# Grouped-query heads of a two-layer diffusion step: four edits to where weight and output splits stand in the order

## The chip, the cores and the metric

The kernel runs on one core of one Trainium2 chip. The metric is the device time of one execution in microseconds, taken as the median of several runs. Beside the timed runs there is one profiled execution, whose trace is read here. Engines are named as in the profile: PE is TensorE, PEld its weight loads, DVE is VectorE, ACT is ScalarE, POOL is GpSimd and SP the engine whose queue issues most DMAs.

## The reference

One step of a transformer with two layers, for 512 latent tokens and 128 context tokens together (640 columns), model width 1024, all in float32. Layer 0 mixes with latent attention and neighbourhood attention, layer 1 with grouped-query attention; a gated feed-forward network follows each. The change lies in layer 1's mixer:

```python
def odd_mixer_latent(h, c_k, c_v, w_in, q_norm, k_norm, w_out, cos, sin):
    b, L, _ = h.shape
    q, k, v = odd_project(h, w_in, q_norm, k_norm)
    q = apply_rope(q, cos, sin)
    k = apply_rope(k, cos, sin)
    o = attend_blocked(q, jnp.concatenate([k, c_k], axis=1), jnp.concatenate([v, c_v], axis=1), GQA_SCALE)
    return o.reshape(b, L, -1) @ w_out
```

There are eight query heads of 128 and two heads of keys and values. `odd_project` multiplies by the input weights and normalises each query and key by its root mean square. The latent tokens read all latent tokens and 128 cached tokens (`c_k`, `c_v`); the context tokens read only themselves.

## The kernel before

Activations lie transposed, features on the 128 partitions and the 640 tokens along the free dimension, in two halves of 320. A float32 product is made of three matmuls: each operand is split into a rounded high part and a rest, and high times high, high times rest and rest times high are added up in PSUM (`mm3`). So every weight tile that arrives by DMA is split before it is used: `unit` (line 168) loads 128x1024 into a raw buffer, ScalarE copies the high part (line 173), VectorE subtracts for the rest (line 174). `rsplit` (line 458) does the same with an activation.

Buffers that matter here: three raw buffers (`rawp`, line 72), each given back when its subtraction is done; three split weight buffers (`wp`, line 73); eight high and eight rest activation tiles (`ring`, line 71).

The order within an engine is made beforehand by a list scheduler: the program order gives each instruction a rank, and the scheduler takes, by its own model of times, the first in rank whose inputs are there. On the chip each engine then runs its list strictly in order. Two helpers bind it further. `after(inst, fn)` (line 177) puts the instructions that `fn` makes for the engine of `inst`, and only those, behind `inst`. `run` (line 115) and `sequence` (line 121) chain pieces on TensorE: each piece's matmuls come behind those of the piece before.

The grouped-query layer goes through these stages:

- Keys. `two_halves` (line 1041) multiplies the two key weights, first for tokens 0 to 319, then for the rest; `knorm` (line 1733) normalises, rotates and splits the keys into `gkh` and `gkl`. The cached keys and values, of 128x256 each, are loaded (lines 1762 and 1765) and split into their places among the keys and values by `ksplit` and `gvsplit`.
- Values. `gvalues` (line 1711) multiplies two value weights, each of four of the eight feature tiles; they are fetched when `gvalues` first asks for them, and their ScalarE copies come behind a step of the activation that feeds the layer (line 1707). The order of the pieces is the list at line 1766.
- Heads. `gqa_q` (line 1782) makes a head's query in eight pieces (`q0` to `q7`), the first four for the first half of the tokens. When a half is done, ScalarE takes it out of PSUM (`gqc`), VectorE rotates it in four instructions (`gqr`), and it is split into `gqh` and `gql`. The sums of squares (`gsq`, then the matmuls `gr`) give the query's scale `rq`. The weight of head h is fetched at the head's first query piece, its ScalarE copy behind the first `gqc` of the head before (line 1783).
- Scores. `gqa_scores` (line 1809) has five blocks: four of 128 latent queries over 640 keys, and a fifth of the context tokens over themselves. Each goes through matmuls (`gs`), a maximum (`gn`), a bias (`gb`) and an exponential (`gp`, line 1833) with its sum, then a scaling on GpSimd. Two PSUM places serve them, so block j+2 waits for the exponential of block j.
- Values of a head. Transposes (`gt`) of the weighed scores are split into `gts_..h` and `gts_..l` and multiplied by the values (`go`); the output goes to `oG`. These pieces of head h run between the scores and queries of head h+1, in the order `GQA_ORDER` (line 1869). Head 7's run by themselves at the end (line 1881).
- Output. The eight outputs are split by `rsplit` (lines 1880 and 1882) into `oGs0` to `oGs7`, and `mixer_out` (line 1049) multiplies eight weights (`ocw0` to `ocw7`), one for each block of 128 output features (`oc0` and so on). The first two output blocks leave the last head's share for later. Between the blocks VectorE makes the last modulation vectors (`junk`, line 1630) from weights `wm` and a broadcast of the conditions (`cbo`), which are loaded on SP's queue among the output weights.

Around the edits the program has these lines:

```python
    ckf = load(cgkT, 256, "gckf")
    for v in range(2):
        ksplit(v, 512, 640, ckf[:, P * v:P * v + P])
    gvsplit(4, load(cgv, 256, "gcvf"))
    run([lambda: gvalues(range(2), range(KT)),
```

Of the kernel before, what the change touches and what calls it, by code (L numbers as in the profile page):

```python
# [13 lines left out]
AF = mybir.ActivationFunctionType  # L14
# [4 lines left out]
P = 128  # L19
# [32 lines left out]
def body(ctx, tc, xT, vecs, crow, wm0, wm0g1, wm0g, wm1, wA, wNV, wNA, wMK, wMV, wOA, wGQ, wGK, wGV, wOC,  # L52
# [3 lines left out]
    V, S, G = nc.vector, nc.scalar, nc.gpsimd  # L56
# [106 lines left out]
    def load(src, n, name):  # L163
        raw = rawp.tile([P, 1024], F32, tag="raw", name=name)
        nc.sync.dma_start(raw[:, :n], src)
        return raw[:, :n]

    def unit(src, n, name, lo="v", pool=None, bufs=3):

        raw = load(src, n, name + "r")  # L170
        t = (pool or wp).tile([P, 2, 1024], F32R, tag="w", bufs=bufs, name=name)
        hi, lw = t[:, 0, :n], t[:, 1, :n]
        S.activation(hi, raw, AF.Copy)
        (V if lo == "v" else G).tensor_tensor(lw, raw, f(hi), ALU.subtract)
        return hi, lw
# [307 lines left out]
    def lazy(fn):  # L483
        box = []

        def get():
            if not box:
                box.append(fn())
            return box[0]
        return get  # L490
# [555 lines left out]
                wh, wl = un(w0)  # L1046
                proj(pss[u][c], wh[0], wh[1], hh, hl, [k], *HALF[c], first=first and j == 0, last=last and j == n - 1, w0=wl)

    def mixer_out(wsrc, os_, order, xin, ml, name, nxt, pre, beside=None, early=False):

        nrm = Norm(name + "n", D)
        oh, ol = [o[0] for o in os_], [o[1] for o in os_]
        x = []
        ks = [(k, k) for k in order]
        if True:
            def wunit(n):
                get = lazy(lambda: unit(wsrc[n], 1024, f"{name}w{n}"))
                return lambda w0: (get(), w0)

            def evac(n, c, ps):  # L1060
                if c == 0:
                    x.append(xin(n))
                residual(x[n], x[n], ps, ml, G1, n, c)
                nrm.add(x[n], c)

            def half(ps, un, c, ks, first=True, last=True):
                two_halves([ps], [un], ks, oh, ol, c, first=first, last=last)

            held = []
            uns = [wunit(n) for n in range(KT)]  # L1070
            for n in range(KT):
                un = uns[n]
                if beside and n >= 1:
                    if early:
                        un(0)
                    beside(n - 1)
                if n < 2:
                    ps = pair(f"{name}{n}")
                    for c in range(2):
                        half(ps, un, c, ks[:-1], last=False)  # L1080
                    held.append((ps, un))
                    if n == 1:
                        for i, (ps, un) in enumerate(held):
                            for c in range(2):
                                half(ps, un, c, ks[-1:], first=False)
                                evac(i, c, ps[c])
                        held = []
                elif n < 5:
                    ps = pair(f"{name}{n}")
                    for c in range(2):  # L1090
                        half(ps, un, c, ks)
                        evac(n, c, ps[c])
                else:
                    ps = pair(f"{name}{n}") if n < 7 else [bank(f"{name}{n}{c}") for c in range(2)]
                    half(ps, un, 0, ks)
                    evac(n, 0, ps[0])
                    held.append((n, ps, un))
            pre()
            for j in range(KT - 2):
                for n, ps, un in held:  # L1100
                    half(ps, un, 1, ks[j:j + 1], first=j == 0, last=False)
                if j >= 1:
                    nxt(x, nrm, 0, (j - 1,))
            for i, (n, ps, un) in enumerate(held):
                half(ps, un, 1, ks[-2:], first=False)
                evac(n, 1, ps[1])
                nxt(x, nrm, 0, (5 + i,))
        return x, lambda: nxt(x, nrm, 1, range(KT))
# [650 lines left out]
    def gvsplit(i, src):  # L1759
        S.activation(gvh[i], src, AF.Copy)  # L1760
        V.tensor_tensor(gvl[i], src, f(gvh[i]), ALU.subtract)
    ckf = load(cgkT, 256, "gckf")
    for v in range(2):
        ksplit(v, 512, 640, ckf[:, P * v:P * v + P])
    gvsplit(4, load(cgv, 256, "gcvf"))
    run([lambda: gvalues(range(2), range(KT)),
         lambda: two_halves(pss, units, allk[:5], hh, hl, 1, last=False),
         lambda: knorm(0),
         lambda: two_halves(pss, units, allk[5:], hh, hl, 1, first=False),
         lambda: ksquare(1),  # L1770
         lambda: gvalues(range(2, 5), range(2)),
         lambda: knorm(1),
         lambda: gvalues(range(2, 5), range(2, KT))])
# [3 lines left out]
    S.activation(gvf[:, :256], gvo[4], AF.Copy)  # L1777
    nc.gpsimd.dma_start(o_gv, gvf[:, :256])

    gqs = {}  # L1780

    def gqa_q(h):
        get = lazy(lambda: after(gqs[h - 1][3][0] if h else None, lambda: unit(wGQ[h], 1024, f"wgq{h}")))
        qh = gp.tile([P, T], F32R, tag="gqh", bufs=2, name=f"gqh{h}")
        ql = gp.tile([P, T], F32R, tag="gql", bufs=2, name=f"gql{h}")
        rq = tiny.tile([P, 5], F32, tag="rq", bufs=2, name=f"rq{h}")
        sq = tmp(f"gsq{h}")
        gqs[h] = qh, ql, rq, []
        out = []
        for c, (c0, c1) in enumerate(HALF):  # L1790
            def done(ps, c=c, c0=c0, c1=c1):
                qc = tp.tile([P, HT], F32, tag="u", bufs=7, name=f"gqc{h}{c}")
                gqs[h][3].append(S.activation(qc, ps[:, :HT], AF.Copy))
                S.activation(sq[:, c0:c1], qc, AF.Square)
                qr = tp.tile([P, HT], F32, tag="u", bufs=7, name=f"gqr{h}{c}")
                rope(qr, qc, vcol(V_GQ), c, f"gqr{h}{c}")
                S.activation(qh[:, c0:c1], qr, AF.Copy)
                V.tensor_tensor(ql[:, c0:c1], qr, f(qh[:, c0:c1]), ALU.subtract)
            out += pieces_of(f"gq{h}{c}", qbank, get, hh, hl, list(range(KT)), c0, c1, done)

        def rstd():
            pr = bank(f"gr{h}")
            for j in range(5):
                PE.matmul(pr[:, 2 * j:2 * j + 2], sq[:, P * j:P * j + P], ones[:, 0:2], start=True, stop=True)
            S.activation(rq, pr[:, 0:10].rearrange("p (a b) -> p a b", b=2)[:, :, 0], AF.Ln, bias=eps, scale=1.0 / P)
            S.activation(rq, rq, AF.Exp, bias=lnsc, scale=-0.5)
        return out + [rstd]

    def gqa_scores(h, pts):
        v = h // 4  # L1810
        ll = tiny.tile([P, 5], F32, tag="lg", bufs=4, name=f"gl{h}")

        def piece(j):
            qh, ql, rq, _ = gqs[h]
            q = qh[:, P * j:P * j + P], ql[:, P * j:P * j + P]
            nm = tiny.tile([P, 1], F32, tag="nm", name=f"gn{h}_{j}")
            nb = tiny.tile([P, 1], F32, tag="nb", name=f"gb{h}_{j}")
            pss = bank2(f"gs{h}_{j}")
            if j < 4:
                pt = gp.tile([P, T], F32, tag="gp", bufs=8, name=f"gp{h}_{j}")  # L1820
                scores(pss, q, kTh[v], kTl[v])
                V.tensor_reduce(nm, pss[:, :, :HT], AX.XY, ALU.max, negate=True)  # L1822
                src, dst, n = pss[:, :, :HT], halves(pt), T
            else:
                pt = gp.tile([P, P], F32, tag="gpp", bufs=1, name=f"gp{h}_{j}")
                src = pss[:, 0, :P]
                mm3(src, *q, kTh[v][:, 640:768], kTl[v][:, 640:768], True, True)
                V.tensor_reduce(nm, src, AX.X, ALU.max, negate=True)
                dst, n = pt, P

            def weigh():
                V.tensor_tensor(nb, nm, rq[:, j:j + 1], ALU.mult)  # L1832
                S.activation(dst, src, AF.Exp, bias=nb, scale=rq[:, j:j + 1], accum_out=ll[:, j:j + 1])  # L1833
                softmax_tail(pt, ll[:, j:j + 1], f"gr{h}_{j}", n)
                pts.append(pt)
            return weigh

        box = []
        rest = {f"s{j}": (lambda j=j: piece(j)()) for j in range(1, 5)}
        return {"s0": lambda: box.append(piece(0)), "x0": lambda: box[0](), **rest}  # L1840
# [29 lines left out]
    for h in range(8):  # L1870
# [4 lines left out]
        if h < 7:  # L1875
# [1 line left out]
            pieces.update(named("q", qp))  # L1877
        sequence(GQA_ORDER, {**pieces, **tail})
        tail = gqa_values(h, pts, oG[h])
    oGs = [rsplit(oG[h], f"oGs{h}") for h in range(7)]  # L1880
    sequence("t0 t1 t2 v0 t3 pt v1 t4 v2 v3 v4 pv", tail)
    oGs.append(rsplit(oG[7], "oGs7"))
    sb.close()
# [3 lines left out]
    box, nxt = next_mod("h11", gs[1][1], mods[1], SH2, op[7])  # L1887
    _, before = mod_side([(1, wm1[G2:], G2)], None)
    x, pend = mixer_out(wOC, oGs, list(range(8)), lambda n, x=x: x[n], mods[1], "oc", nxt, op[-1],
                        before(op[5], op[5], (2, 1, 1, 2, 1, 1, 0)), True)  # L1890

    def final(x, nrm, c, ks, root):
        c0, c1 = HALF[c]
# [167 lines left out]
```

## Time and profile before

| | us |
|---|---|
| median of 3 runs | 1498.22 (1497.03 to 1499.88) |
| profiled execution, whole | 1497.4 |
| profiled execution, from first to last instruction (span) | 1495.3 |
| mean granted clock of TensorE in it | 0.996 |
| first matmul of the keys | 823.3 |
| first score matmul of head 0 | 863.8 |
| last query matmul of head 7 | 986.1 |
| first matmul of the output projection | 1001.0 |

How to read the lines quoted below. A row of a timeline gives the start in microseconds from the start of the span, the duration, the engine (PEq, SPq for a queue that issues a DMA), the line of the program, the operation, the tile written and the tiles read, the shape, the number of such instructions merged into the row, and in brackets the idle time of the engine before it with what ended it. Matmuls overlap: a matmul of 128x320 takes 0.31 us by its row while one starts every 0.15. A row of a table of windows gives a stretch of the span, its length, the busy time of PE, PEld, DVE, ACT and POOL with the number of instructions, the granted clock of TensorE, the share of DMA time and the GB/s.

### The profile page before, as it was taken

What the parts mean: (1) busy time and instruction counts of PE and PEld (TensorE: products, weight loads), DVE (VectorE), ACT (ScalarE), POOL (GpSimd) and SP (SyncE); (2) the same over time, 40 slices, a digit from 0 to 9 for tenths busy, and PEclk for the clock granted to TensorE, in tenths of its full rate; (3) what the DMA queues carried; (4) which work ended last, traced back from release to release, by engine and by line L of the source; (5) the groups of instructions that cost most, each with busy time, mean ns of one, the idle gap of its engine ahead of it and who ended that gap; (6) DMA issues with size and microseconds to landing.
All of it is one profiled execution on the core that took longest, in us unless ns stands there. A gap on an engine that the chain in (4) does not pass through costs nothing. (4 is left out here: it accounts for less than half of the span.)

```text
span 1495.3 us, 25840 instructions
## 1 busy us (share of the span) xinstructions
PE 1448.1 (97%) x9766; PEld 1391.3 (93%) x9766; DVE 1235.8 (83%) x2378; ACT 786.6 (53%) x1542; POOL 178.0 (12%) x272
## 2 busy tenths in 40 slices
PE   6999989999999999999999999999999999999997
PEld 4989978889899999999999999989899999999997
DVE  5877788877878898956898878887899989889976
ACT  5446677753745555541223656672565555655443
POOL 0046636420000000000000122220100000000000
PEclk9999999999999999999999999999999999999999
DMA  9653341025164544559664210115145555548571
GB/s 372 207 151 123 114 145 44 15 95 174 47 216 154 166 166 166 164 197 343 225 218 167 92 46 30 42 40 184 60 164 172 190 173 191 176 152 297 179 265 71
DMA packets 79635, 231.47 MB, mean 155 GB/s; under 512 B 8856, under 2 KB 13240, under 8 KB 79128
## 3 DMA queue, kind: packets, MB, share of 16 engines
q1 hardware_dynamic: 77152, 225.43, 43.8%
q10 hardware_dynamic: 1944, 3.48, 0.7%
q8 instruction: 76, 1.25, 0.3%
q0 software_dynamic: 416, 0.93, 0.2%
q14 instruction: 47, 0.39, 0.1%
HBM read 193.15 MB, written 36.66 MB: 154 GB/s over the span
## 5 line engine op out<-in xcount | busy, mean ns | idle before, releaser
L1630 DVE SCALAR_TENSOR_TENSOR junk<-wm,cb 128x1024 bf16<-128x1024 f32 x88 | 107.4, 1220 | 2.4 <-DMA wm<-in_wm 1.8
L64 PE MATMUL gq<-h10h,wgq 128*128 128x320 f32 x256 | 66.5, 319 | 0.0
L261 POOL TENSOR_SCALAR h10h<-h10t,gs,mods 128x320 fp32r<-128x320 f32 x4 | 3.2, 790 | 436.7 <-DVE h10t L255 434.4
L1370 ACT ACTIVATE wY<-s 128x1024 fp32r<-128x1024 f32 x37 | 39.2, 1060 | 27.7 <-PE fg L64 24.0
L1896 POOL TENSOR_TENSOR xr<-xw,fn1rs 128x320 f32<-128x320 f32 x2 | 1.7, 862 | 416.9 <-ACT fn1rs L229 416.9
L1370 ACT ACTIVATE wZ<-s 128x1024 fp32r<-128x1024 f32 x37 | 39.1, 1057 | 18.7 <-PE fd L64 16.1
L1479 DVE TENSOR_TENSOR sg<-up,sg 128x640 f32<-128x640 f32 x37 | 30.5, 823 | 20.9 <-ACT sg L1478 19.8
L1371 DVE TENSOR_TENSOR wZ<-s,wZ 128x1024 fp32r<-128x1024 f32 x37 | 45.2, 1223 | 2.9 <-ACT wZ L1370 0.2
L64 PEld LDWEIGHTS gq<-h10h,wgq 128*128 128x128 f32 x256 | 45.5, 191 | 0.6
L1371 DVE TENSOR_TENSOR wY<-s,wY 128x1024 fp32r<-128x1024 f32 x37 | 45.1, 1219 | 0.3
L1478 ACT ACTIVATE sg<-fg 128x320 f32<-128x320 f32 x37 | 16.2, 439 | 48.6 <-PE fg L64 48.6
L64 PE MATMUL fg<-h01q,wgu 128*128 128x320 f32 x192 | 40.3, 316 | 0.9 <-ACT h01q L298 0.5
L1500 ACT ACTIVATE p<-fd 128x320 f32<-128x320 f32 x37 | 16.2, 438 | 46.6 <-PE fd L64 46.6
L1833 ACT ACTIVATE gp<-gs,gb,rq 128x640 f32<-128x640 f32 (+1 forms) x40 | 31.8, 795 | 16.5 <-DVE gb L1832 13.3
L64 PE MATMUL gq<-h10l,wgq 128*128 128x320 f32 x128 | 39.8, 311 | 0.0
L64 PE MATMUL fg<-h11q,wX 128*128 128x320 f32 x228 | 36.7, 309 | 0.0
L64 PE MATMUL fu<-h11q,wX 128*128 128x320 f32 x228 | 36.6, 308 | 0.0
L64 PE MATMUL fd<-h11q,wZ 128*128 128x320 f32 x228 | 36.6, 309 | 0.0
L64 PE MATMUL fg<-h11E,wW 128*128 128x320 f32 x228 | 36.5, 309 | 0.0
L64 PE MATMUL fg<-h11N,wZ 128*128 128x320 f32 x228 | 36.5, 309 | 0.0
L64 PE MATMUL fd<-h11D,wY 128*128 128x320 f32 x228 | 36.4, 308 | 0.0
L64 PE MATMUL fg<-h11C,wY 128*128 128x320 f32 x228 | 36.4, 308 | 0.0
(3425 smaller groups left out, 5327.3 us busy)
## 6 DMA issues: line engine op xcount, KB each, us to landing
wm<-in_wm SPq DMA_DIRECT2D x48, 512.0 KB, 4.3
mraw<-in_wm SPq DMA_DIRECT2D x8, 1024.0 KB, 13.1
mraw<-in_wm SPq DMA_DIRECT2D x16, 512.0 KB, 3.6
wmv<-in_wm0g SPq DMA_DIRECT2D x8, 512.0 KB, 4.1
wm<-in_wm0g SPq DMA_DIRECT2D x8, 512.0 KB, 4.4
ruo<-in_wFO SPq DMA_DIRECT2D x8, 512.0 KB, 3.5
rgo<-in_wFO SPq DMA_DIRECT2D x8, 512.0 KB, 6.1
x<-in_xT SPq DMA_DIRECT2D x8, 320.0 KB, 5.5
```

The source lines that it names most:

```text
L64: cls.last = nc.tensor.matmul(*a, **k)
L261: G.tensor_scalar(h[:, c0:c1], t, self.gsl[:, k, 0:1], self.ml[:, self.sh + k, 0:1], ALU.mult, ALU.add)
L1370: S.activation(h, src, AF.Copy)
L1371: V.tensor_tensor(w_, src, f(h), ALU.subtract)
L1478: last = S.activation(sg[:, 0:HT], g[:, :HT], AF.Silu, scale=-1.0)
L1479: V.tensor_tensor(sg, up, sg, ALU.mult)
L1500: S.activation(p5, b5[:, :HT], AF.Copy)
L1630: V.scalar_tensor_tensor(junk, raw, 1.0, cb[:, c, :], ALU.mult, ALU.mult, accum_out=mods[l][:, j0 + i, c:c + 1])
L1833: S.activation(dst, src, AF.Exp, bias=nb, scale=rq[:, j:j + 1], accum_out=ll[:, j:j + 1])
L1896: G.tensor_tensor(x[k][:, c0:c1], root[1][k], nrm.rs[:, c0:c1], ALU.mult)
```

## The change

Four edits, all of them to order; no arithmetic is added or taken away.

1. The loading and splitting of the cached keys and values becomes a function, called as a piece behind `ksquare(1)` instead of ahead of the list. The loads of the two values' weights now come before it in program order.
2. The ScalarE copy of head 1's query weight is no longer put behind head 0's first `gqc`; heads 2 to 7 keep theirs. (The new argument `lo` has the same value either way and is what `unit` takes by default.)
3. The ScalarE copies of the output splits of heads 3 to 6 are put behind the exponential of head 7's fourth block, the last of the latent tokens.
4. The ScalarE copy of the third output weight (`ocw2`) is put behind the same exponential. For that `mixer_out` has a new argument `hold`, which layer 0's call doesn't use.

```diff
-    def mixer_out(wsrc, os_, order, xin, ml, name, nxt, pre, beside=None, early=False):
+    def mixer_out(wsrc, os_, order, xin, ml, name, nxt, pre, beside=None, early=False, hold=None):
...
             def wunit(n):
-                get = lazy(lambda: unit(wsrc[n], 1024, f"{name}w{n}"))
+                get = lazy(lambda: after(hold if n == 2 else None, lambda: unit(wsrc[n], 1024, f"{name}w{n}")))
...
-    ckf = load(cgkT, 256, "gckf")
-    for v in range(2):
-        ksplit(v, 512, 640, ckf[:, P * v:P * v + P])
-    gvsplit(4, load(cgv, 256, "gcvf"))
+    def cached():
+        ckf = load(cgkT, 256, "gckf")
+        for v in range(2):
+            ksplit(v, 512, 640, ckf[:, P * v:P * v + P])
+        gvsplit(4, load(cgv, 256, "gcvf"))
     run([lambda: gvalues(range(2), range(KT)),
          lambda: two_halves(pss, units, allk[:5], hh, hl, 1, last=False),
          lambda: knorm(0),
          lambda: two_halves(pss, units, allk[5:], hh, hl, 1, first=False),
          lambda: ksquare(1),
+         cached,
          lambda: gvalues(range(2, 5), range(2)),
...
-        get = lazy(lambda: after(gqs[h - 1][3][0] if h else None, lambda: unit(wGQ[h], 1024, f"wgq{h}")))
+        get = lazy(lambda: after(gqs[h - 1][3][0] if h > 1 else None, lambda: unit(wGQ[h], 1024, f"wgq{h}", lo="v" if h == 1 else "v")))
...
-                S.activation(dst, src, AF.Exp, bias=nb, scale=rq[:, j:j + 1], accum_out=ll[:, j:j + 1])
+                gexp[h, j] = S.activation(dst, src, AF.Exp, bias=nb, scale=rq[:, j:j + 1], accum_out=ll[:, j:j + 1])
...
-    oGs = [rsplit(oG[h], f"oGs{h}") for h in range(7)]
+    oGs = [after(gexp[7, 3] if h > 2 else None, lambda: rsplit(oG[h], f"oGs{h}")) for h in range(7)]
...
-                        before(op[5], op[5], (2, 1, 1, 2, 1, 1, 0)), True)
+                        before(op[5], op[5], (2, 1, 1, 2, 1, 1, 0)), True, hold=gexp[7, 3])
```

More of the change, by code (lines that the diff above doesn't have):

```diff
@@ L1778, in body @@
     nc.gpsimd.dma_start(o_gv, gvf[:, :256])
-    gqs = {}
+    gqs, gexp = {}, {}
     def gqa_q(h):
-        get = lazy(lambda: after(gqs[h - 1][3][0] if h else None, lambda: unit(wGQ[h], 1024, f"wgq{h}")))
+        get = lazy(lambda: after(gqs[h - 1][3][0] if h > 1 else None, lambda: unit(wGQ[h], 1024, f"wgq{h}", lo="v" if h == 1 else "v")))
         qh = gp.tile([P, T], F32R, tag="gqh", bufs=2, name=f"gqh{h}")
```

## The prediction

> **What bounds the kernel now.** I read the page's first part, then a table of windows over the grouped-head layer, then TensorE's waits, then each engine in order of time around them.
>
> ```profile
> span 1495.3 us, 25840 instructions
> PE 1448.1 (97%) x9766; PEld 1391.3 (93%) x9766; DVE 1235.8 (83%) x2378; ACT 786.6 (53%) x1542; POOL 178.0 (12%) x272
> ```
>
> ```profile
> 823.30:855.60 32.30, 31.42 (x227) 30.29 (x226) 27.58 (x61) 20.31 (x47) 5.42 (x9) 1.00 0.30 105
> 855.60:870.00 14.40, 13.52 (x85) 13.25 (x84) 10.36 (x22) 6.76 (x17) 0.54 (x1) 0.88 0.14 51
> ...
> 939.00:957.00 18.00, 18.00 (x126) 17.21 (x125) 14.49 (x33) 11.34 (x28) 3.69 (x6) 1.00 0.09 30
> ...
> 975.00:993.00 18.00, 16.94 (x116) 15.84 (x115) 16.28 (x35) 14.95 (x33) 4.96 (x5) 1.00 0.01 2
> 993.00:1015.00 22.00, 20.91 (x128) 18.14 (x128) 13.20 (x29) 11.19 (x25) 4.49 (x5) 1.00 0.37 126
> ```
>
> The first fence is the page's head. A row of the table of windows gives the window, its length, then the busy time of TensorE, its weight loads, VectorE, ScalarE and GpSimd, the granted clock and the DMAs. TensorE is busy 97% of the span, so only an idle stretch of TensorE is worth anything. A middle head (939 to 957) has none. The windows that the change touches lack 0.88, 0.88, 1.06 and 1.09 us. In the last head's (975 to 993) ScalarE and VectorE are at 14.95 and 16.28 of 18, against 11.34 and 14.49 in a middle head: there the side engines hold TensorE up. The idle time is these stops of TensorE:
>
> ```profile
> 834.98 0.39 PE L64 MATMUL gvp<-wgv,h10h 128*128 128x256 f32 x1 [0.88 <-DVE wgv L174]
> ...
> 863.84 0.55 PE L64 MATMUL gs<-gkh,gqh 128*128 128x320 f32 x2 [0.88 <-ACT gqh L1797]
> ...
> 989.02 0.83 PE L64 MATMUL gr<-ones,gsq 128*128 128x2 f32 x6 [0.38 <-ACT gsq L1794]
> 992.77 0.56 PE L64 MATMUL gs<-gkh,gqh 128*128 128x320 f32 x2 [0.68 <-ACT gp L1833]
> 995.67 0.56 PE L64 MATMUL gs<-gkh,gqh 128*128 128x320 f32 x2 [0.62 <-ACT gp L1833]
> 998.27 0.33 PE L64 MATMUL gs<-gkh,gqh 128*128 128x128 f32 x1 [0.32 <-ACT gp L1833]
> ```
>
> Together 3.76 us: 0.88 for the second values' weight, 0.88 for head 0's first query, 2.00 in head 7's scores. That is the ceiling of what the edits can win by taking waits away; the clock, below, can add to it.
>
> **Cached keys and values behind the first values' weights.** The edit adds no work. It moves two loads, three ScalarE copies and three VectorE subtractions behind the two loads of the values' weights, on SP's queue and in priority.
>
> ```profile
> 811.13 0.33 SPq L165 DMA_DIRECT2D gcvf<-in_cgv  x1
> ...
> 828.32 0.33 SPq L165 DMA_DIRECT2D wgv1r<-in_wGV  x1
> ...
> 827.27 0.40 ACT L1760 ACTIVATE gvh<-gcvf 128x256 fp32r<-128x256 f32 x1
> ...
> 828.05 1.05 ACT L173 ACTIVATE wgv<-wgv0r 128x1024 fp32r<-128x1024 f32 x1
> ...
> 827.81 0.48 DVE L1731 TENSOR_TENSOR gkl<-gckf,gkh 128x128 fp32r<-128x128 f32 x2
> 828.22 0.41 DVE L1761 TENSOR_TENSOR gvl<-gcvf,gvh 128x256 fp32r<-128x256 f32 x1
> ...
> 833.71 1.22 DVE L174 TENSOR_TENSOR wgv<-wgv1r,wgv 128x1024 fp32r<-128x1024 f32 x1
> ```
>
> The second values' weight is asked for at 828.32, as soon as the cached keys' subtraction (827.81 to 828.29) gives its raw buffer back, and the first weight's copy stands behind the cached values' copy. With the cached loads behind, the two weights take the places of the cached loads on the queue, the last of which went at 811.13, so both are in place long before 828. The first copy can start up to 0.78 earlier (828.05 - 827.27) and its subtraction, then without 0.48 + 0.41 of cached work ahead, about as much. The second weight's subtraction, which follows in the same chain, then ends some 0.8 earlier against a stop of 0.88. Bounds: 0 (the side engines keep the old order) and 0.88; I take 0.8, since nothing but the copies stands between. The cached work has to go somewhere later: 0.89 on VectorE. Its cover is in the next fence: VectorE idles 2.44 before 844.02. Without cover it would delay the keys' rotation by 0.89. On SP's queue the loads of the query weights now stand behind the cached loads, and those behind the first values' weight giving its buffer back; the query comes after all of the keys' and values' matmuls, which cover a load that is some microseconds later.
>
> **Head 1's weight no longer behind head 0's query.** One copy and one subtraction leave the stretch between head 0's query and its scores.
>
> ```profile
> 844.02 0.55 DVE L1741 SCALAR_TENSOR_TENSOR kn<-gk0a,vec,krs 128x320 f32<-128x320 f32 x1 [2.44 <-ACT krs L1740]
> 859.94 0.55 DVE L1699 SCALAR_TENSOR_TENSOR gqr<-gqc,vec,tg 128x320 f32<-128x320 f32 x1 [1.21 <-ACT gqc L1793]
> ...
> 861.65 1.23 DVE L174 TENSOR_TENSOR wgq<-wgq1r,wgq 128x1024 fp32r<-128x1024 f32 x1
> 862.79 0.49 DVE L1702 TENSOR_TENSOR gqr<-gqr,gqr00b 128x320 f32<-128x320 f32 x1
> ```
>
> Here the subtraction (861.65) sits between the rotation's products and its sum: without it the sum starts 1.14 earlier (862.79 - 861.65), more than the stop of 0.88. The subtraction itself fits VectorE's gap of 1.21 before 859.94; without that cover, it delays the rotation again by 1.14 and nothing is won. Next behind the score matmuls come the small sums of squares, which wait for the query's second half; they can give some of it back. Bounds -0.9 (the cached work's 0.89 lands in the same gap and the stop grows by it) to 0.88; I take 0.7, near the upper end because the gap has its size.
>
> **The clock behind that stop.** Right after it the trace shows a stretch at half clock:
>
> ```profile
> 866.00:867.00 1.00, 1.00 (x5) 1.00 (x6) 1.00 (x2) 0.57 (x2) 0.00 (x0) 0.50 0.00 0
> ...
> 868.00:869.00 1.00, 1.00 (x5) 1.00 (x5) 0.00 (x0) 0.53 (x2) 0.00 (x0) 0.50 0.02 8
> 869.00:870.00 1.00, 1.00 (x8) 1.00 (x7) 0.67 (x1) 0.00 (x0) 0.00 (x0) 0.81 0.00 0
> ```
>
> Of these rows of 1 us each the first and the last of three at 0.50 are shown, and the next. The missing shares of clock add to 3 x 0.50 + 0.19 = 1.7 us. The stops of head 7 left the clock at 1.00 (993 to 1015), so a stop alone doesn't bring this; the stop together with the small matmuls behind it did, once. Bounds 0 and 1.7; one profiled execution can't say in how many runs it occurs, so I count half, 0.85. [...]
>
> **Four output splits and the third output weight behind head 7's last latent scores.** Held are the ScalarE copies of heads 3 to 6 and of weight 2; their subtractions follow them by data.
>
> ```profile
> 986.61 0.73 ACT L461 ACTIVATE oGs4h<-oG 128x640 fp32r<-128x640 f32 x1
> ...
> 987.55 1.05 ACT L173 ACTIVATE ocw<-ocw2r 128x1024 fp32r<-128x1024 f32 x1
> 988.50 0.46 ACT L1794 ACTIVATE gsq<-gqc 128x320 f32<-128x320 f32 x1
> ...
> 991.33 0.82 DVE L462 TENSOR_TENSOR oGs5l<-oG,oGs5h 128x640 fp32r<-128x640 f32 x1
> 995.93 1.21 DVE L174 TENSOR_TENSOR ocw<-ocw2r,ocw 128x1024 fp32r<-128x1024 f32 x1
> 997.05 0.16 DVE L1832 TENSOR_TENSOR gb<-gn,rq 128x1 f32<-128x1 f32 x1
> ...
> 1005.90 0.60 ACT L390 ACTIVATE gts_3h<-gt 128x512 fp32r<-128x512 f32 x1 [1.41 <-PE gt L68]
> 1009.99 0.60 ACT L1862 ACTIVATE oG<-go 128x512 f32<-128x512 f32 x1 [1.54 <-PE go L64]
> ```
>
> Each stop of head 7 has one of these ahead of it. The squares start 0.95 later for the weight's copy (988.50 - 987.55) and the stop is 0.38; the exponential's bias at 997.05 stands behind 1.12 us of the weight's subtraction and the stop is 0.32. Of the held work, head 6's copy comes behind the scores anyway; heads 3, 4, 5 and the weight come to about 3 x 0.73 + 1.05 = 3.2 us of ScalarE and 3 x 0.82 + 1.21 = 3.7 of VectorE in a stretch where both are nearly full. Taken out, these engines have a middle head's load less the work for a next query, and a middle head runs the same scores on the same two banks without a stop (939 to 957), though with query matmuls between. 2.00 are to be had, of which I take 1.9. They return behind the last scores. ScalarE's two gaps shown there hold 2.95, and TensorE has output matmuls of heads 0 to 2, which stay unheld, to fill with: cost 0, bound 2.0 (all given back) without that cover. The copy of weight 2 holds a raw buffer longer, so the load of weight 5 and what stands behind it on SP's queue come later; that is the slower rival below.
>
> **Sum.** 0.8 + 0.7 + 1.9 = 3.4, with half of the clock's stretch 4.25 us. The profiled execution took 1497.4 (span 1495.3 and 2.1 around it), so 1493.15 by its own account. The median of the runs is 1498.22, 0.8 above it, and it is what counts: 1498.2 - 4.25 = 1494.0.
>
> **Rivals.** *Freed work comes back on the keys' chain.* ScalarE's copy of head 1's weight (1.05, as for any such weight) or its subtraction (1.23) lands ahead of the keys' squares or rotations instead of in the gaps; the first two gains go. For it: an engine's order is fixed beforehand and doesn't bend to what runs late. Against it: the gaps (2.44 and 1.21) exceed the 2.1 us to be placed. Only head 7's 1.9 remains: 1496.3. Chance 0.12.
>
> *The held splits delay head 7's own values.* They stand earlier in the program than the last head's transposes, so they may go ahead of the copies that TensorE waits for, up to 3.2 us, and give back the 2.0. For it: their higher rank. Against it: the gaps and the unheld outputs. 1498.2 - 1.5 = 1496.7. Chance 0.08.
>
> *Slower: the third weight holds SP's queue.* This needs rows of its own:
>
> ```profile
> 997.20 0.33 SPq L165 DMA_DIRECT2D ocw5r<-in_wOC  x1
> 1007.07 0.33 SPq L1639 DMA_DIRECT2D cbo<-crs  x1
> ...
> 1011.55 0.83 DVE L462 TENSOR_TENSOR oGs7l<-oG,oGs7h 128x640 fp32r<-128x640 f32 x1 [2.39 <-ACT oGs7h L461]
> 1016.74 1.23 DVE L1630 SCALAR_TENSOR_TENSOR junk<-wm,cbo 128x1024 bf16<-128x1024 f32 x1
> 1021.17 0.55 DVE L324 SCALAR_TENSOR_TENSOR xr<-oc0a,mods,xr 128x320 f32<-128x320 f32 x1 [3.20 <-PE oc0a L64]
> ```
>
> The load of weight 5 follows weight 2's subtraction (995.93 + 1.21), and behind it on the queue stand the condition vectors (1007.07), for which VectorE's modulation products wait. If the subtraction slips behind the last head's (1011.55 + 0.83), all 3.4 us earlier, it ends at 1010.2 and the vectors go at 1010.5 instead of 1003.7, 6.8 late; three products then end at 1017.97 - 3.4 + 6.8 = 1021.4, while the first output block wants VectorE at 1017.8. TensorE stands 3.6, and another half-clock stretch costs 1.7: 1498.2 - 3.4 + 5.3 = 1500.1. It decides from where the subtraction ends later than some 1007, the gap of 3.20 being used up. Against it: VectorE has 2.39 free before 1011.55. Chance 0.12.
>
> **Numbers.** The forecast has 0.68, with a range of its own from 1491.5 (everything at its upper bound and the clock in full, 3.76 + 1.7, and 1.2 for the spread of the runs, which were 1.2 below to 1.7 above their median) to 1496. From what a measurement can tell, 0.2% or 3.0 us, faster means below 1495.2: nearly all of the forecast, 0.68 with the rivals' edges. The two weak rivals give 0.20 for within, the queue 0.12 for slower. The range 1491.0 to 1499.0 holds the forecast and both weak rivals and leaves the slow one out.
>
> **What would show it.** Right: the stops at 834.98, 863.84 and the four of head 7 gone or under 0.2 us, no half clock before 870, the values' weights asked for by 812, and weight 2's copy behind head 7's fourth exponential. Wrong: a new stop at the keys' norm matmuls, at the first score, at head 7's values after 1000, or at the third output block, with the condition vectors issued late.

## The result and the profile after

The changed kernel took 1495.08 us (median of 22 runs, 1491.14 to 1498.08) against 1498.28 for 22 runs of the kernel before beside them: a ratio of 0.9975, 95% interval 0.9969 to 0.9981, or 2.8 to 4.6 us. Forecast were 1494.0, with a chance of 0.68 for faster. The profiled execution of after took 1495.92, its span 1494.1.

To compare the two traces in their own time, the layer is cut at its own matmuls: A from the first value matmul to head 0's first query matmul, B from there to head 0's first score, C to head 1's first score, D from head 7's first score to the third output block. These are the windows of before and of after, in the order A, B, C, D (length, then busy time of PE, PEld, DVE, ACT, POOL, granted clock, DMA share, GB/s):

```profile
830.95:855.76 24.81, 23.93 (x178) 22.98 (x177) 20.88 (x47) 15.46 (x37) 4.09 (x7) 1.00 0.27 94
855.76:863.84 8.08, 7.20 (x51) 6.93 (x49) 6.22 (x14) 3.96 (x11) 0.54 (x1) 1.00 0.05 17
863.84:878.22 14.38, 14.07 (x86) 13.53 (x86) 10.59 (x25) 7.69 (x18) 3.56 (x4) 0.88 0.11 38
987.21:1022.29 35.08, 32.94 (x213) 29.83 (x213) 22.95 (x46) 17.39 (x39) 5.11 (x6) 1.00 0.31 106
```

```profile
834.14:858.09 23.95, 23.76 (x178) 22.93 (x177) 20.44 (x43) 15.01 (x37) 4.55 (x7) 1.00 0.35 110
858.09:865.12 7.03, 7.03 (x50) 6.96 (x49) 5.69 (x15) 3.19 (x10) 0.54 (x1) 1.00 0.12 43
865.12:878.13 13.01, 12.61 (x87) 12.00 (x86) 10.39 (x25) 7.90 (x18) 3.54 (x4) 1.00 0.01 2
987.13:1020.66 33.53, 32.80 (x213) 29.74 (x213) 23.77 (x46) 17.77 (x39) 4.27 (x5) 1.00 0.29 111
```

A is 0.86 shorter, B 1.05, D 1.55: 3.46 us together. Between C and D nothing differs (108.99 before, 109.00 after), nor between the first key matmul and A (7.60 and 7.57). C differs by 1.37, and there the clock is the difference: 0.88 against 1.00.

The stops of TensorE answer to those of before. These are rows of after's timeline of TensorE: a stop at the keys' norm, head 0's first score, then the two stops left in the last head:

```profile
850.49 0.81 PE L64 MATMUL gkp<-ksq,ones 128*128 128x320 f32 x2 [0.19 <-ACT ksq L1727]
...
865.12 0.52 PE L64 MATMUL gs<-gkh,gqh 128*128 128x320 f32 x2
...
994.05 0.56 PE L64 MATMUL gs<-gkh,gqh 128*128 128x320 f32 x2 [0.23 <-ACT gp L1835]
...
1000.02 0.33 PE L64 MATMUL gop<-gtp6l,gvh 128*128 128x128 f32 x1 [0.34 <-DVE gtp6l L391]
```

The stop of 0.88 at the values is gone, head 0's first score has none (no bracket), and the four of head 7 (2.00) have become 0.23 and 0.34. The side engines and SP's queue show why (same kernel, timelines of SP, ACT and DVE):

```profile
813.36 0.33 SPq L165 DMA_DIRECT2D wgv0r<-in_wGV  x1
814.54 0.33 SPq L165 DMA_DIRECT2D wgv1r<-in_wGV  x1
...
1005.89 0.37 SPq L1639 DMA_DIRECT2D cbo<-crs  x1
...
848.71 1.05 ACT L173 ACTIVATE wgq<-wgq1r 128x1024 fp32r<-128x1024 f32 x1
...
850.02 0.41 ACT L1727 ACTIVATE ksq<-gk0b 128x320 f32<-128x320 f32 x1
...
997.77 0.73 ACT L461 ACTIVATE oGs3h<-oG 128x640 fp32r<-128x640 f32 x1
...
1003.10 1.07 ACT L173 ACTIVATE ocw<-ocw2r 128x1024 fp32r<-128x1024 f32 x1
```

```profile
835.01 1.22 DVE L174 TENSOR_TENSOR wgv<-wgv1r,wgv 128x1024 fp32r<-128x1024 f32 x1
...
853.76 1.22 DVE L174 TENSOR_TENSOR wgq<-wgq1r,wgq 128x1024 fp32r<-128x1024 f32 x1
...
862.33 0.55 DVE L1699 SCALAR_TENSOR_TENSOR gqr<-gqc,vec,tg 128x320 f32<-128x320 f32 x1 [0.68 <-ACT gqc L1795]
...
864.04 0.49 DVE L1702 TENSOR_TENSOR gqr<-gqr,gqr00b 128x320 f32<-128x320 f32 x1
...
998.54 1.17 DVE L462 TENSOR_TENSOR oGs3l<-oG,oGs3h 128x640 fp32r<-128x640 f32 x1 [0.34 <-ACT oGs3h L461]
...
999.70 0.27 DVE L391 TENSOR_TENSOR gtp6l<-gtp,gtp6h 128x128 fp32r<-128x128 f32 x1
...
1004.22 1.22 DVE L174 TENSOR_TENSOR ocw<-ocw2r,ocw 128x1024 fp32r<-128x1024 f32 x1
```

The second values' weight is asked for at 814.54, not at 828.32 (the keys' first matmul comes 3.2 us later in this trace, so on the clock of before that is 811.3, by the 812 that the prediction named), and its subtraction starts 0.87 behind the first value matmul (835.01 - 834.14) where it was 2.76 behind (833.71 - 830.95). Head 1's subtraction stands at 853.76, in the keys' rotation; the query's sum follows its last product without it (864.04). Its copy on ScalarE (848.71) stands ahead of the keys' squares (850.02), which is the new stop of 0.19. In the last head, head 3's subtraction (998.54, 1.17 long) stands ahead of the rest `gtp6l` that TensorE waits for: the new stop of 0.34. The condition vectors go at 1005.89, 1.2 earlier than before.

### The profile page after: what moved, and what is told of

Read it like the earlier page. It is cut to its first block, busy times and chain, and to the rows that moved or that the text cites. A ratio compares the mean times of both kernels' runs of the same rounds, so it can differ in the third digit from the quotient of the medians.

```text
span 1494.1 us, 25843 instructions
## 1 busy us (share of the span) xinstructions
PE 1448.7 (97%) x9766; PEld 1392.5 (93%) x9766; DVE 1235.9 (83%) x2378; ACT 785.7 (53%) x1542; POOL 178.0 (12%) x272
## 3 DMA queue, kind: packets, MB, share of 16 engines
q8 instruction: 76, 1.25, 0.3%
## 4 chain that ended last, share of the span: by engine, by line
PE 77%; DVE 10%; ACT 6%; DMA 4%; issue 2%; POOL 0%; DVEq 0%; ACTq 0%; SPq 0%; POOLq 0%
PE fg L64 19%; PE fd L64 9%; PE fgo L64 5%; PE fu L64 4%; PE gq L64 3%; PE fdo L64 3%; PE fo L64 2%; DVE junk L1630 2%; PE gs L64 2%; PE go L64 2%; PE nk L64 2%; PE nq L64 2%; PE fuo L64 1%; PE gt L68 1%; PE mod L64 1%
```

## The experiments

Two theories were held against each other. *Stops*: each edit wins the stops that it was meant for, and the half clock behind head 0's first score comes and goes by chance. *Clock*: the half clock belongs to the kernel before and is a large part of the gain. In the table below, "clock lost" is the sum of (1 - granted clock) over rows of 1 us around head 0's first scores.

**Both kernels again.** No edit.

> The kernel before once more, unchanged, for a second profile and the granted clock of each run. Stretches of its first profile: A, from the first value matmul to head 0's first query matmul, 24.81 us; B, from there to head 0's first score, 8.08; C, from there to head 1's first score, 14.38; D, from head 7's first score to the third output block's first matmul, 35.08. Stops theory (each edit wins the stops it takes away, the clock only sometimes adds): A, B and D within 0.1 of these, C either near 14.4 with a half-clock stretch of 1.7 or near 12.7 without. Clock theory (the half-clock stretch at head 0 belongs to every run of before, and its loss is a large part of the gain): C again near 14.4. Time 1498.3.

> The changed kernel once more, unchanged. Its first profile: A 23.95, B 7.03, C 13.01, D 33.53. Both theories: the same within 0.1, no half clock at head 0, and time 1495.1. The stop of 1.37 at the last norm of layer 0, which lies ahead of all edits, is chance by both and should be gone or different.

**The edits in two pairs.** `e12` has the cached keys' move and head 1's weight, `e34` the four splits and the third output weight, each with the other pair's lines as before.

> The first two edits alone (cached splits behind, head 1's weight free). Stops theory: A 23.95 and B 7.03 as in the changed kernel, D 35.08 as before, so 1.9 us less than before and up to 1.7 more where before has the half clock: 1496.4 to 1495.6. Clock theory: as much as the whole change less a little, 1495.5.

> The last two edits alone (four output splits and the third output weight held). Stops theory: A 24.81 and B 8.08 as before, D 33.5, so 1.5 us less than before: 1496.8. Clock theory: hardly any gain in time, since the half clock at head 0 stays: 1498.

| | A | B | C | D | clock lost | runs, median us | ratio, interval |
|---|---|---|---|---|---|---|---|
| before | 24.81 | 8.08 | 14.38 | 35.08 | 1.71 | | |
| b_again | 24.81 | 8.07 | 14.12 | 35.05 | 1.71 | 1498.32 | 1.0000, 0.9987 to 1.0012 |
| after | 23.95 | 7.03 | 13.01 | 33.53 | 0 | 1495.08 | 0.9975, 0.9969 to 0.9981 |
| a_again | 23.95 | 7.03 | 12.99 | 33.56 | 0 | 1494.08 | 0.9978, 0.9968 to 0.9989 |
| e12 | 23.95 | 7.03 | 13.01 | 35.05 | 0 | 1496.34 | 0.9992, 0.9981 to 1.0004 |
| e34 | 24.81 | 8.07 | 12.93 | 33.58 | 0 | 1496.05 | 0.9991, 0.9981 to 1.0001 |

A, B and D come out the same to 0.05 us in every profile, and each pair wins its own stretches and nothing else. The two pairs add up. C goes with the clock and not with the edits: `e34` still has its stop of 0.88 ahead of head 0's first score, and yet 12.93 and no clock lost. That speaks against the clock theory in its strong form. The runs can't tell the pairs apart: each is worth under 2 us, and both intervals reach to about no change. The stop of 1.37 in the first trace of after is not in the second, as expected.

**One edit at a time.** `e1` has the function `cached` alone; `e2` alone

```diff
-        get = lazy(lambda: after(gqs[h - 1][3][0] if h else None, ...
+        get = lazy(lambda: after(gqs[h - 1][3][0] if h > 1 else None, ...
```

> Only the cached keys and values are moved behind the first values' weights. Stops theory, each edit wins its own stop: first value matmul to head 0's first query matmul 23.8 to 23.95 us (24.81 before), head 0's query to its first score stays at 8.07, the last head's stretch at 35.05. Rival, the moved work comes back on VectorE ahead of the keys' rotation: the first stretch shortens by less than 0.3, with a new stop at the keys' norm or at the first score.

> Only head 1's weight is freed from head 0's query; the cached keys stay ahead of the values' weights. Stops theory, each edit wins its own stop: first value matmul to head 0's first query matmul stays 24.81 us (up to 0.2 more for a stop at the keys' norm, if ScalarE's copy of the weight lands ahead of the keys' squares), head 0's query to its first score goes from 8.07 to 7.03, the last head's first score to the third output block stays at 35.05. Rival, the two first edits need each other (the freed work only fits where the cached work has left): the first stretch grows by 0.5 to 1 us, or the second stays at 8.07.

`e1` has A 23.69 (23.8 to 23.95 were expected), B 8.07, D 35.06; `e2` A 25.09, B 7.03, D 35.06. These are the window A of `e1`, then the window A of `e2` and its stop at the keys' norm:

```profile
830.60:854.29 23.69, 23.69 (x179) 22.94 (x177) 20.33 (x46) 14.77 (x36) 4.53 (x7) 1.00 0.29 96
```

```profile
832.81:857.90 25.09, 24.03 (x178) 22.99 (x177) 21.25 (x46) 15.98 (x38) 4.07 (x7) 1.00 0.31 107
```

```profile
850.29 1.07 PE L64 MATMUL gkp<-ksq,ones 128*128 128x320 f32 x3 [0.18 <-ACT ksq L1727]
```

The cached keys' move wins 1.12 in A (24.81 - 23.69). Freeing head 1's weight costs 0.28 in A, by the copy ahead of the keys' squares, and wins 1.05 in B: 0.77 net. Together 1.12 - 0.28 is the 0.84 of A in both (0.86). The rival that the two need each other is out: `e2` alone takes the whole stop from B. And a stop costs more than its idle time, 1.12 and 1.05 for 0.88 each. A matmul that need not wait starts before the one ahead of it has ended (a row of 0.31 for each 0.15, as said above), and by the author's estimate a stop loses that overlap too: 0.88 + 0.16 is 1.04. That fits the 1.05 and leaves 0.08 of the 1.12 open; no run tests it by itself.

**The last head, splits and weight apart.** `e3` holds the four splits alone, `e4` the third output weight alone:

```diff
+    oGs = [after(gexp[7, 3] if h > 2 else None, lambda: rsplit(oG[h], f"oGs{h}")) for h in range(7)]
```

```diff
+                get = lazy(lambda: after(hold if n == 2 else None, lambda: unit(wsrc[n], 1024, f"{name}w{n}")))
```

> Only the four output splits are held behind head 7's fourth exponential; the third output weight keeps its place. Stops theory: of the last head's stops those behind the splits go (0.68 and 0.62) and those behind the weight's copy and subtraction stay (0.38 and 0.32); the stretch from the last head's first score to the third output block goes from 35.05 to some 33.9, if the new stop of 0.34 at the values of the last head comes with the splits. Rival, the weight's copy and subtraction set all four stops since they are the last in the chain: the stretch stays within 0.3 us of 35.05.

> Only the third output weight is held; the four splits keep their places. Stops theory: the stops of 0.38 and 0.32 go, those of 0.68 and 0.62 stay, and the stretch from the last head's first score to the third output block goes from 35.05 to some 34.4. Rival, the weight is the whole cause: 33.55, as with both. A third outcome, that the splits spread over the time that the weight leaves and the stops only move: 35.05.

D is 34.71 in `e3` and 34.58 in `e4`: 0.37 and 0.50 won, 0.87 together, where both at once win 1.55. The forecasts of 33.9 and 34.4, which gave each held group its own stops, both missed, that of `e3` by 0.8. Head 7's first exponential shows why. It starts 4.55 us behind the head's first score in before, 4.92 in `e3`, 4.54 in `e4` and 3.38 in after, and the third score block needs the PSUM place that it sets free. These are its rows in before and in after, then rows of `e3` (ACT, DVE, PE), then of `e4`:

```profile
991.76 0.87 ACT L1833 ACTIVATE gp<-gs,gb,rq 128x640 f32<-128x640 f32 x1
```

```profile
990.51 0.88 ACT L1835 ACTIVATE gp<-gs,gb,rq 128x640 f32<-128x640 f32 x1
```

```profile
990.00 0.89 ACT L1833 ACTIVATE gp<-gs,gb,rq 128x640 f32<-128x640 f32 x1
...
986.55 1.23 DVE L174 TENSOR_TENSOR ocw<-ocw2r,ocw 128x1024 fp32r<-128x1024 f32 x1
987.69 0.48 DVE L1702 TENSOR_TENSOR gqr<-gqr,gqr71b 128x320 f32<-128x320 f32 x1
...
991.04 0.56 PE L64 MATMUL gs<-gkh,gqh 128*128 128x320 f32 x2 [1.60 <-ACT gp L1833]
998.45 0.33 PE L64 MATMUL gop<-gtp6h,gvh 128*128 128x128 f32 x1 [0.60 <-ACT gtp6h L390]
```

```profile
986.71 0.72 ACT L461 ACTIVATE oGs4h<-oG 128x640 fp32r<-128x640 f32 x1
987.34 0.42 ACT L1793 ACTIVATE gqc<-gq 128x320 f32<-128x320 f32 x1
...
991.86 0.87 ACT L1833 ACTIVATE gp<-gs,gb,rq 128x640 f32<-128x640 f32 x1
...
987.70 0.90 DVE L462 TENSOR_TENSOR oGs4l<-oG,oGs4h 128x640 fp32r<-128x640 f32 x1
...
992.87 0.56 PE L64 MATMUL gs<-gkh,gqh 128*128 128x320 f32 x2 [1.21 <-ACT gp L1833]
```

In `e3` what is not held moves up into the room that the splits leave: the weight's subtraction goes ahead of the rotation's sum (986.55; before, it stood at 995.93, far behind it), and the first exponential is late. One stop of 1.60 takes the place of the four, and the held splits bring stops of 0.60 and 0.19 at head 7's values. In `e4` nothing moves up there. The splits of heads 3 and 4 stand where they stood in before, ahead of `gqc` and of the rotation, so the first exponential comes no earlier, and the stops of 0.38 and 0.68 become one of 1.21. What `e4` wins are the later stops (0.62 and 0.32), less one of 0.32 at the first output block. Only with both groups held is the way to the first exponential free.

**Held one block longer.** The whole change, with the splits behind `gexp[7, 4]`:

```diff
-    oGs = [after(gexp[7, 3] if h > 2 else None, ...
+    oGs = [after(gexp[7, 4] if h > 2 else None, ...
```

> The whole change, with the four splits held behind the fifth exponential of head 7 (the last score block, of the cached keys) instead of the fourth. If the new stop of 0.34 at the last head's values is the price of the third head's split standing ahead of the last exponential's tail on VectorE, it goes, and the stretch from the last head's first score to the third output block shortens from 33.55 to some 33.2. If the splits are then late for what follows (the output matmuls of heads 3 to 6, or the residual's sum behind the first output block), a stop of 0.3 to 2 us shows there, between the third output block and the FFN or ahead of it, and the stretch does not shorten.

(The fifth block is that of the context tokens, not of the cached keys.) The stop of 0.34 goes, as the reading of 998.54 said, but stops of 0.21 and 0.20 come in its place, and D stays at 33.56. The output stage from the third block to the first feed-forward matmul takes 46.53 instead of 43.63. Rows of its VectorE, then one stop of TensorE:

```profile
1010.86 1.22 DVE L1630 SCALAR_TENSOR_TENSOR junk<-wm,cbo 128x1024 bf16<-128x1024 f32 x1 [1.85 <-DMA wm<-in_wm]
...
1016.48 0.55 DVE L324 SCALAR_TENSOR_TENSOR xr<-oc0a,mods,xr 128x320 f32<-128x320 f32 x1 [4.39 <-PE oc0a L64]
...
1027.97 0.41 PE L64 MATMUL oc3a<-oGs0h,ocw 128*128 128x320 f32 x1 [1.03 <-DVE ocw L174]
```

VectorE makes one modulation product, then idles for 4.39 us until the first output block; after makes three there (1014.52 to 1018.21) and idles 1.25. The products that fell behind crowd the residual's sums and the output weights' subtractions, and TensorE stands 0.45, 1.03 and 0.44 for these. The list made beforehand is different, and the rows follow it (one product ahead of 1016.48, where after has three ahead of 1019.54): the slower rival's price at the rival's place, but by the list's order and not by a late load. Some of the 2.90 comes back, since the feed-forward then waits less for its input: from the first key matmul to the feed-forward's last wait for it are 257.30 us, against 255.23 in after and 260.00 in before (of which 1.4 are the half clock in C). One block of difference in a hold gives back 2.07 of the 3.46. The run took 1496.20.

**One more weight freed.** The whole change, with `h > 2` in place of `h > 1` in the condition of the head weights.

> The whole change, and head 2's weight freed from head 1's query as well. Stops theory: the two stops of 0.25 and 0.26 at head 1's first scores stand behind that weight's copy and subtraction, as head 0's stood behind head 1's; they go, and head 0's first score to head 1's first score shortens from 13.01 by 0.25, the time to head 7's first score by 0.5. If the freed work lands ahead of head 0's query or softmax, a stop of 0.2 to 0.9 comes up there and the whole from first value matmul to head 7's first score is the same or longer.

```profile
852.00 1.06 ACT L173 ACTIVATE wgq<-wgq2r 128x1024 fp32r<-128x1024 f32 x1 [0.75 <-PE gvp L64]
...
854.59 1.23 DVE L174 TENSOR_TENSOR wgq<-wgq2r,wgq 128x1024 fp32r<-128x1024 f32 x1
...
863.65 0.56 PE L64 MATMUL gs<-gkh,gqh 128*128 128x320 f32 x2 [0.38 <-ACT gqh L1799]
```

A third query weight's subtraction (854.59) now stands in the keys' rotation, which has no more room (the gap of 0.68 ahead of the query's rotation is gone), and 0.38 of head 0's stop is back. B is 7.57 (0.54 lost), the time from head 1's to head 7's first score 108.48 (0.52 won), D 33.83 (0.30 lost); C is 12.96, so the 0.25 expected there did not come; the whole from the first key matmul to the feed-forward 238.02 against 237.72. By these stretches neither `hold4` nor `free2` beats the change itself; their single runs, 1496.20 and 1495.90, can't tell.

**A longer stop.** The kernel before, with the subtraction of head 1's weight computed three times:

```diff
+        for _ in range(3 if name == "wgq1" else 1):
+            (V if lo == "v" else G).tensor_tensor(lw, raw, f(hi), ALU.subtract)
```

> The kernel before, with the subtraction of head 1's weight computed three times in place of once, so that some 2.3 us more (two times 1.14) stand on VectorE between the rotation's products of head 0's query and its sum, and the stop of 0.88 grows to some 3.2. Stops theory: the runs' mean grows by about 2.3 us above before, the stretch from head 0's query to its first score from 8.07 to some 10.4, and a half-clock stretch may or may not stand behind the stop. Clock theory: a longer stop always brings the half-clock stretch behind it, so head 0's first score to head 1's first score takes 14.2 or more in place of 12.93, and the runs' mean grows by more than 3.5 us.

The runs took 1502.88 us, ratio 1.0028, interval 1.0018 to 1.0038. The stop did not grow where it was expected: the second and third subtraction were ordered behind the rotation, B stayed at 8.07 with its stop of 0.88, and TensorE stands for 2.07 more at head 1's query. Row of TensorE, then rows of 1 us windows:

```profile
872.18 0.90 PE L64 MATMUL gq<-h10h,wgq 128*128 128x320 f32 x2 [2.07 <-DVE wgq L175]
```

```profile
870.00:871.00 1.00, 0.12 (x1) 0.00 (x0) 1.00 (x4) 0.36 (x3) 0.00 (x0) 0.62 0.00 0
871.00:872.00 1.00, 0.00 (x0) 0.00 (x0) 1.00 (x1) 1.00 (x2) 0.00 (x0) 0.50 0.00 0
...
888.00:889.00 1.00, 1.00 (x6) 1.00 (x5) 0.78 (x4) 0.69 (x3) 0.00 (x0) 0.50 0.11 45
```

The half clock begins inside the stop and loses 3.41 us up to 877, and 1.71 more between 887 and 891, behind stops of 0.33 and 0.26. This is so in the mean of the runs: span times (1 - mean granted clock) is 9.46 +/- 0.51 us over 10 runs, against 6.68 +/- 0.69 over the 13 runs of before beside them and 5.94 +/- 0.30 over all 61. Of the 4.1 us by which the mean time grew over those 13 (1503.17 - 1499.08), some 2.8 +/- 0.9 are clock. C takes 17.59.

So this kernel pays the clock as a rule, and in numbers that is what the clock theory forecast (C 14.2 or more, over 3.5 us in the mean); the 2.3 of the stops theory is too low. But it is no test of the stop of 0.88, which stayed as it was, and it does not say which stop pays. By estimate the half clock begins at 870.24 (0.76 us of the row of 870 at half clock give its 0.62), when the stop of 2.07 is 0.13 us old, so that stop alone can hardly have brought it. In layer 0, in the row of 430 to 440, TensorE idles 2.16 us in `free2` and 2.23 in `e2`, both at a clock of 1.00, and 2.19 in a_again, where the clock is 0.83 and 1.7 us are lost. For the stop of 0.88 the next part has the numbers.

## Why the prediction was right, and which term was off

**Waits.** The sum without the clock was 3.4; the stretches show 3.46. By edit: the cached keys' move 0.8 forecast, 1.12 measured by itself; head 1's weight 0.7 forecast, 0.77 net; the held work 1.9 forecast, 1.55. The first two were bounded by the stop's idle time, 0.88, which is not its whole price: the first passed its bound, and the 3.76 of all the stops together was no ceiling. That the sum came within 0.06 is luck in part, since 0.4 too little there and 0.35 too much in the last head cancel. In the last head 0.23 stayed and 0.34 was new, at head 7's values, where the list of wrong signs looked for one: the first held split went ahead of the rest `gtp6l`. The cost of 0 for the work that returns was wrong by that. Each of head 7's stops was read as the price of the one piece of held work ahead of it. `e3` and `e4` show that they don't divide so: alone the two groups win 0.37 and 0.50, and pricing them as one block was needed.

**Cover.** The subtraction of head 1's weight didn't go into the gap of 1.21 before 859.94, as the step had it, but into the keys' rotation (853.76). There it was covered too, and the gap itself shrank to 0.68. The copy of the same weight was the small new stop at the keys' norm. Freeing one weight more (`free2`) shows the limit of that cover. Nor did the cached work go into the gap of 2.44 ahead of the keys' rotation, which is 2.06 in after: its subtractions stand at 830.75, 833.81 and 838.58, among the steps that make the layer's input.

**The clock.** Half of 1.7 was counted, 0.85. This is the mis-sized term. Leaving out `stall`, where the longer stop follows, six profiles have the stop of 0.88 ahead of head 0's first score, and three of them (before, b_again, e4) the half clock behind it, e1, e3 and e34 not; none of the other six (after, a_again, e12, e2, hold4, free2, where that stop is gone or 0.38) has it. That would be the half that was counted. But the runs don't show it: clock lost per run is 5.94 +/- 0.30 us over 61 runs of before and 6.06 +/- 0.32 over 34 of after, a gain of -0.1 +/- 0.4 (in the profiled execution of before 2.3 us, in that of after 3.5, lie behind TensorE's last matmul, where no matmul is left to slow), and the means, 1498.29 and 1494.62, differ by 3.67 +/- 0.37, which is the waits' 3.46 with little more. These rows of before, of after and of b_again show where such stretches fall else:

```profile
22.00:27.00 5.00, 4.21 (x27) 2.97 (x28) 4.66 (x12) 3.30 (x8) 0.00 (x0) 0.66 1.02 407
198.00:208.00 10.00, 8.14 (x56) 6.52 (x56) 8.14 (x28) 8.75 (x23) 4.93 (x6) 1.00 0.55 189
865.00:870.00 5.00, 5.00 (x27) 5.00 (x28) 2.85 (x6) 1.90 (x5) 0.00 (x0) 0.66 0.11 45
```

```profile
22.00:27.00 5.00, 4.18 (x27) 2.91 (x28) 4.63 (x12) 3.30 (x8) 0.00 (x0) 0.66 1.03 410
198.00:208.00 10.00, 9.54 (x48) 8.52 (x49) 7.20 (x25) 7.12 (x18) 4.33 (x5) 0.66 0.58 179
864.00:872.00 8.00, 7.85 (x55) 7.52 (x54) 5.74 (x15) 4.26 (x10) 0.96 (x2) 1.00 0.00 1
```

```profile
22.00:27.00 5.00, 4.15 (x35) 3.11 (x36) 4.28 (x12) 3.47 (x7) 0.00 (x0) 1.00 1.02 408
198.00:206.00 8.00, 8.00 (x39) 7.64 (x36) 6.40 (x19) 6.34 (x16) 3.14 (x4) 0.57 0.49 166
867.00:871.00 4.00, 4.00 (x18) 4.00 (x19) 2.19 (x6) 1.90 (x5) 0.00 (x0) 0.57 0.01 3
```

Before loses 1.7 at 22 and at 865, after 1.7 at 22 and 3.4 at 198, far ahead of the edits; b_again has it at 198 and 867 and not at 22. The same kernel thus gains or loses several us from run to run, and the profile of after (span 1494.1) hides part of its gain by the 3.4 at 198 and by the stop of 1.37 at the last norm of layer 0. How often the stop of 0.88 draws a stretch is not settled: three of six profiles say half, the runs say less than 0.8 us on average (two standard errors above -0.1). The forecast of 1494.0 is 1.1 below the median, most of it this 0.85.

**The rivals.** Freed work on the keys' chain: 0.28 of it came, not the 1.5 (A of `e2`). Held splits ahead of head 7's values: 0.34 of 2.0. The third weight did not hold SP's queue: its subtraction ended at 1005.44 (1004.22 + 1.22), under the point of some 1007 from which it would have decided, and the condition vectors left early. That VectorE's order in the output stage is as tight as that rival had it shows in `hold4`.

## What to carry to other kernels

- Several pieces of side work can stand in one chain. Hold one, and another moves up into its room (`e3`) or still blocks the way (`e4`): hold them all at once, and try the parts alone before naming one as the cause (0.37 and 0.50 alone, 1.55 together).
- Cut the trace at the kernel's own matmuls and compare the stretches. They came out the same to 0.05 us from profile to profile where whole runs spread over 7 us, and so a gain of 0.8 us can be read from one profile that many runs don't resolve.
- A stretch at half clock seen once in one profile is not a cost to be removed in full: take a second profile, and the mean clock of many runs, before it goes into the sum.

## What the hardware showed

Clock was lost in portions here. The losses found ahead of TensorE's last matmul are 1.70 and 1.71 us in before (from 22 and 865), 1.71 and 3.41 in after (from 22 and 200), 3.42 and 1.7 in b_again (from 198 and 867), 1.7 in a_again (in the row of 430 to 440): each is one or two stretches of 3.4 us at half clock (1.7 / 0.50). Where they fall changes from run to run of the same kernel. The stop of 0.88, with 1.17 us of two-column matmuls soon behind it (864.82 in before), was followed by one three times of six. The stops at or just ahead of the stretches were 1.14 us (up to 22.79) and 0.88 (up to 863.84) in before, 1.19 (up to 22.82) and 1.66 (up to 198.46) in after, and `stall`, whose longest added stop is 2.07, lost some 2.8 us more of clock in the mean of ten runs. What sets a stretch off was not shown.

A stop's price was not its idle time: 0.88 us idle cost 1.05 in one place and 1.12 in another.
